# SyncE's reads in program order and apart, and 72 TensorE transposes replaced by transposing reads

## The chip, the cores and the metric

The kernel runs on one core of a Trainium2 chip. The metric is device time in microseconds of one execution; smaller is better. TensorE is called PE, VectorE DVE, ScalarE ACT, GpSimd POOL and SyncE SP, as in the profile.

## The reference

One decoder layer, 256 tokens of width 2048, in float32. Cut to what matters:

```python
h = x + 0.5 * swiglu(rmsnorm(h, ffn1_norm), ffn1_w_gu, ffn1_w_down)
proj = rmsnorm(h, mix_norm) @ w_in                      # columns: gating u, v | z | x, B, C | dt
gu, gv, z, xbc, dt_raw = jnp.split(proj, split_at, axis=-1)
a_out = chunked_sgu(gelu(gu), gelu(gv), ...)            # u * (W_s rmsnorm(v) + b), chunks of 128
xbc = silu(causal_dwconv(xbc, conv_w, conv_b))          # 4 taps
xs, bm, cm = jnp.split(xbc, ...)                        # 32 heads of 64; 8 groups of 128 states
xdt = x * dt[..., None]                                 # inside ssd_scan, chunks of 128
y = ssd_scan(x, dt, a, bm, cm) + d_skip[:, None] * x
m_out = rmsnorm(y * silu(z), norm_w)
h = h + concat([a_out, m_out]) @ w_out
h = h + cross_attention(rmsnorm(h, xa_norm), rmsnorm(mem, mem_norm), w_q, w_kv, w_o)
h = h + 0.5 * swiglu(rmsnorm(h, ffn2_norm), ffn2_w_gu, ffn2_w_down)
return rmsnorm(h, final_norm)
```

## The kernel before

Every weight matrix is streamed from DRAM in tiles of 1 MB (`raw`, 128 x 2048 floats), one per step of the planner. ACT casts a tile to its high part (`hi`), DVE subtracts to get the low part (`lo`), and PE multiplies both by a token operand that is kept in SBUF, in two forms again. Three `raw` buffers and two `lo` buffers go round: a weight read waits for DVE to have finished the tile three steps back, and a low part for PE to have finished the one two steps back. The stages follow one another on PE: FFN 1, the input projection `w_in` (B, C and x columns by `proj_feat`, features on the partitions, 16 + 16 steps of 5.6 us; then v, u and z columns by `proj_tok`, tokens on the partitions, 48 steps of 5.45 us), the output projection `w_out`, cross attention, FFN 2. In `w_out` and the FFNs, pieces of kind "S" share products between sums of operands, so that DVE also forms sums of the weights (`sum`) and of the operand (`forms`, `mts`, `ats`).

Work beside the matmuls is put off by `later(fn, by=n)`: it is issued n steps of the planner later, between two weight steps. PE's instructions, ACT's casts and the low parts on DVE (`split_op`) are each kept in program order; the other instructions are placed on their engine by a scheduler.

Turning an operand (tokens on the partitions to features on the partitions, or back) is done in two ways. Either PE multiplies by the identity (`tpose`, L77) into PSUM, and ACT or DVE copy from there. Or `write_planes` lets ACT split the floats into two planes of 16 bits (`halves`), POOL's queue writes these to DRAM (`planes`), and SP's queue reads them back with a transposing DMA (`turned`, L375). The weight reads stand on SP's queue too, where the scheduler places the transposing reads among them.

The x features come out of the convolution as `xf` (4 multiply-adds on DVE and one product on ACT into `cacc`, then silu on ACT), and are turned to token rows `y0`, `y1` by `x_tokens`. `scan_start` (L875) multiplies y by dt into `xdt` and y by the skip weights; `scan_decay` forms the decays and the scores; `scan_apply` adds PE's `yp` to y. `m_operand` scales y by the norm's factor and turns it into the second half of the operand of `w_out` (`mt`, and `mts` with the sums); `ats.turn_later` does so for the gating output; `Normed.chunk` for the residual stream that the next stage reads (`na` for attention).

Of the kernel before, what the change touches and what calls it, by code (L numbers as in the profile page):

```python
# [47 lines left out]
def hybrid_layer(ctx: ExitStack, tc: tile.TileContext, x, xt, mem, memt, w_gu1, w_dn1, w_in, w_s, w_out,  # L48
# [84 lines left out]
    PLAIN = {(0, 0): 0, (0, 1): 1, (1, 0): 2, (1, 1): 3}  # L133
    FOR_SUMS = {(0, 0): 0, (1, 0): 1, (1, 1): 2, (0, 1): 3}

    def load(w, r0, cs, at, fine=False):
        raw = wraw.tile([P, 2 * KP, NC], F32, name="raw")
        rows = w[r0:r0 + KP * P, :]
        if at is PLAIN and cs[1] == cs[0] + NC:
            nc.sync.dma_start(out=raw.rearrange("p (k j) n -> p k j n", j=2), in_=rows[:, cs[0]:cs[0] + 2 * NC].rearrange(  # L140
                "(k p) (j n) -> p k j n", p=P, j=2))
            return raw
        if fine:
            for (k, j), b in at.items():
                nc.sync.dma_start(out=raw[:, b, :], in_=rows[k * P:(k + 1) * P, cs[j]:cs[j] + NC])
            return raw
        for j, c in enumerate(cs):
            b, e = at[0, j], at[1, j]
            src = rows[:, c:c + NC]
            if e > b:  # L150
                nc.sync.dma_start(out=raw[:, b:e + 1:e - b, :], in_=src.rearrange("(k p) n -> p k n", p=P))
                continue
            for k, x in enumerate((b, e)):
                nc.sync.dma_start(out=raw[:, x, :], in_=src[k * P:(k + 1) * P, :])
        return raw

    def behind(instructions):

        order = ExitStack()
        for ins in instructions:  # L160
            order.enter_context(tc.issue_after(ins))
        return order
# [161 lines left out]
    def proj_feat(w, xts, n0):  # L324
        ps = {}
        n = D // P // (2 * KP)
        for i in range(n):
            raw = wraw.tile([P, 2 * KP, NC], F32, name="raw")
            nc.sync.dma_start(out=raw, in_=w[2 * i * KP * P:2 * (i + 1) * KP * P, n0:n0 + NC].rearrange(
                "(k p) n -> p k n", p=P))  # L330
# [40 lines left out]
            nc.gpsimd.dma_start(out=planes[t * P:(t + 1) * P].rearrange("p b n -> p (b n)"), in_=halves)  # L371
        return planes

    def read_turned(to, planes, c0, n):
        nc.sync.dma_start(out=to, in_=planes[:, :, c0:c0 + n].rearrange("s b n -> (s b) n"), transpose=True)  # L375

    def turn_over(srcs, by, put):
        planes = write_planes(srcs)

        def fetch(q):  # L380
            to = half_k(F32, "turned")
            read_turned(to.bitcast(U16).rearrange("p (k s) -> p k s", k=KP), planes, q * P, KP * P)
            later(lambda: put(to.rearrange("p (k s) -> p k s", k=KP), q), by=by[1], bankless=True)

        for q in (0, 2):
            later(lambda q=q: fetch(q), by=by[0] + q / 4, bankless=True)

    def in_turn(src, last, op, c0=None):

# [66 lines left out]
    class Pieces(dict):  # L456
# [59 lines left out]
                                             op=ALU.subtract)  # L516
            return hi.ins, lo.ins

        def turn_later(self, srcs, by, c0=None, at=None):
            if at is None:  # L520
                at = self.due
                self.due += 2
            turn_over(srcs, by, lambda to, q: self.put(at + q // 2, to, q, c0))

        def later(self, srcs, c0=None, by=1):
            for q in (0, 2):
# [2 lines left out]
    class Normed:  # L529
# [8 lines left out]
        def chunk(self, n, by=1):  # L538
            srcs = [h[n][:, t, :] for t in range(NT)]
            if n < 2 and not isinstance(self.xts, Pieces):  # L540
                operand_turned(srcs, self.xts, f"xt_{self.name}{n}", self.c0 + n * KG, (2.5 + 1.5 * n, 2.5))
                self.stats(n)
            elif isinstance(self.xts, Pieces):

                for i in (2 * n, 2 * n + 1):
                    later(lambda i=i: self.xts.put(i, srcs, i % 2 * KP, self.c0 + n * KG),
                          self.bys.get(i, by))
                later(lambda: self.stats(n), self.stats_by)
            else:
                operand_later(srcs, self.xts, f"xt_{self.name}{n}", self.c0 + n * KG, by)  # L550
                self.stats(n)
# [59 lines left out]
    def ffn(nrm, w_gu, w_dn, done=None, each=None, fine=0, by_token=False):  # L611
        for c_from, c_to in ((0, 5), (5, 11)):
            kinds, turn = DN_KINDS[c_to - c_from]
            hts = Pieces(kinds, "hid", nrm.xts)
            for c in range(c_from, c_to):
                m = {}
                gs = []

                def mid(banks):
                    m["m1"], m["y"], m["z"], m["y2"] = parts_of(banks)  # L620

                def evac(t, j, ps):
                    g, u = (m["z"], m["y2"]) if t else (m["m1"], m["y"])
                    if j == 0:
                        total(g, ps, g, ALU.subtract if t else ALU.add)
                        nc.scalar.activation(g, g, AF.Silu, scale=nrm.rstd[:, t:t + 1])
                        return
                    total(u, ps, u)
                    nc.vector.scalar_tensor_tensor(out=g, in0=u, scalar=nrm.rstd[:, t:t + 1], in1=g,
                                                   op0=ALU.mult, op1=ALU.mult)  # L630
                    gs.append(g)

                if c == 0:
                    proj_sum(w_gu, 0, nrm.xts, FIRST_KINDS, (c * NC, DFF + c * NC), mid, evac, FIRST, fine)
                else:
                    proj_sum(w_gu, 0, nrm.xts, GU_KINDS, (c * NC, DFF + c * NC), mid, evac, GU_ORDER)
                hts.turn_later(gs, (1, 4))
            last = c_to == 11
            add_sum(w_dn, c_from * NC, hts, (kinds, kinds), turn, 0.5, done if last else None, each if last else None,
                    last and by_token)  # L640

# [186 lines left out]
    bt = slot([P, GROUPS, S], F32, "bt")  # L828
    ctr = slot([P, GROUPS, S], F32, "ct")
    def b_tokens(q):  # L830
        ps = side("tpose")
        for i in range(4):
            transpose(out=ps[:, i * P:(i + 1) * P], in_=bt[:, q * 4 + i, :P], identity=ident)
        nc.any.tensor_copy(out=btok[:, q * 4:q * 4 + 4, :], in_=ps.rearrange("p (g n) -> p g n", n=P))

    for c in range(4):
        xis = gather(proj_feat(w_in, nx.xts, B0 + c * NC))
# [3 lines left out]
        for i in range(4):  # L841
            conv_silu(xis[i], 16 + c * 4 + i, dst[:, (c % 2) * 4 + i, :])
        if c < 2:
            later(lambda c=c: b_tokens(c), by=2)
    y = [slot([P, HEADS, HD], F32, f"y{t}") for t in range(NT)]

    def x_tokens(c, i0, xf):
        tps = side("tpose").rearrange("p (t k s) -> p t k s", t=NT, k=2)
        for t in range(NT):
            for i in range(2):  # L850
                transpose(out=tps[:, t, i, :], in_=xf[:, i, t * P:(t + 1) * P], identity=ident)
        for t in range(NT):
# [12 lines left out]

    def per_head(ap, n):
# [5 lines left out]
    def scan_start(t, j):  # L872
        if j == 0:
            scan["xdt"] = scan[f"xdt{t}"] = xdt = slot([P, HEADS, HD], F32, "xdt")
            nc.vector.tensor_tensor(out=xdt, in0=y[t], in1=per_head(dt[:, t, :], HD), op=ALU.mult)  # L875
            nc.vector.tensor_tensor(out=y[t], in0=y[t], in1=per_head(rowb[:, 2, :], HD), op=ALU.mult)
        dec = slot([P, 16, P], F32, "dec")
        nc.gpsimd.dma_start(
# [98 lines left out]
    for c in (0, 2):  # L977
# [41 lines left out]

# [205 lines left out]
```

## Time and profile before

| | before |
|---|---|
| median of 3 runs | 2428.43 us (2428.28 to 2432.98) |
| profiled execution | 2428.32 us, span 2426.6 us |
| PE busy | 2413.6 us, 99% of the span |
| DVE / ACT / POOL busy | 2033.3 / 1361.4 / 65.4 us |
| matmuls on PE | 11141 |
| granted TensorE clock | 0.999 |
| DMA | 510.17 MB, mean 210 GB/s |

The span is the profiled execution without the 1.7 us around it. Busy times are sums of one engine's instructions; PE's matmuls overlap, so that what one costs on PE's path is read from the distance of their starts or from the chain, not from its own duration.

### The profile page before, as it was taken

The numbers are of one execution on the slowest core, as the hardware profiler recorded it, in microseconds if no ns is written. First come the engines' busy times: TensorE is split into PE (matmuls) and PEld (weight loads), VectorE is DVE, ScalarE is ACT, GpSimd is POOL, SyncE is SP. The second block draws the span as 40 slices with busy tenths as digits, with TensorE's granted clock in tenths as the row PEclk, the third lists the DMA queues.
The fourth block names the chain that finished last, engine by engine and source line by source line (L and its number), as shares of the span: only waits on it lengthen the run. The fifth ranks groups of instructions, "written<-read, shape, count | busy, mean of one in ns | idle before, by whom it ended". The sixth has DMA issues, their size and how long they took to land.

```text
span 2426.6 us, 29016 instructions
## 1 busy us (share of the span) xinstructions
PE 2413.6 (99%) x11141; PEld 2010.1 (83%) x11141; DVE 2033.3 (84%) x1943; ACT 1361.4 (56%) x1261; POOL 65.4 (3%) x124
## 2 busy tenths in 40 slices
PE   9999999999999999999999999999999999999998
PEld 7888888888888888788888888888888888888886
DVE  8999889999877777655698888778899988899997
ACT  7565446555656555445555655555556644556554
POOL 1000000000000000000000000000000000000000
PEclk9999999999999999999999999999999999999999
DMA  8777667677765555567557655555567776777774
GB/s 306 234 225 232 202 208 232 220 231 231 232 196 187 181 191 175 205 194 224 190 191 244 224 191 167 176 178 174 191 217 235 225 222 197 223 229 223 233 221 151
DMA packets 264844, 510.17 MB, mean 210 GB/s; under 512 B 75760, under 2 KB 77840, under 8 KB 263936
## 3 DMA queue, kind: packets, MB, share of 16 engines
q1 hardware_dynamic: 256224, 479.00, 62.6%
q0 software_dynamic: 7648, 28.26, 3.2%
q8 instruction: 87, 1.43, 0.2%
q10 hardware_dynamic: 832, 1.05, 0.1%
q14 instruction: 53, 0.43, 0.0%
HBM read 476.76 MB, written 16.81 MB: 203 GB/s over the span
## 4 chain that ended last, share of the span: by engine, by line
PE 95%; issue 3%; ACT 1%; DVE 1%; DMA 0%; SPq 0%; POOL 0%; POOLq 0%; DVEq 0%; ACTq 0%
PE acc L74 92%; PE tpose L77 1%; PE yp L74 1%; PE o L74 0%; PE logits L74 0%; PE mixed L74 0%; DVE lo L177 0%; DMA raw<-in_w_in 0%; ACT hi L169 0%; DMA raw<-in_w_gu 0%; PE dt L74 0%; PE scores L74 0%; PE yo L74 0%; PE st L74 0%; ACT hi L191 0%
## 5 line engine op out<-in xcount | busy, mean ns | idle before, releaser
L177 DVE TENSOR_TENSOR lo<-raw,hi 128x2048 fp32r<-128x2048 f32 (+2 forms) x449 | 945.2, 2107 | 242.5 <-PE acc L74 175.4
L169 ACT CAST hi<-raw 128x2048 fp32r<-128x2048 f32 (+1 forms) x437 | 785.0, 1798 | 488.6 <-PE acc L74 418.4
L74 PE MATMUL acc<-hi,xp_ffn 128*128 128x512 f32 x1824 | 574.3, 390 | 0.0
L74 PEld LDWEIGHTS acc<-hi,xp_ffn 128*128 128x128 f32 x1824 | 342.6, 188 | 71.1
L169 ACT CAST hi<-sum 128x2048 fp32r<-128x2048 f32 x117 | 224.1, 1915 | 294.8 <-DVE sum L177 153.4
L74 PE MATMUL acc<-lo,xp_ffn 128*128 128x512 f32 x912 | 355.0, 389 | 1.3 <-DVE h L661 1.3
L177 DVE TENSOR_TENSOR lo<-sum,hi 128x2048 fp32r<-128x2048 f32 x117 | 268.1, 2292 | 37.4 <-ACT hi L169 37.4
L74 PE MATMUL acc<-hi,hid 128*128 128x512 f32 x896 | 281.3, 389 | 0.0
L74 PE MATMUL acc<-hi,xt_mix 128*128 128x512 f32 x768 | 241.5, 393 | 0.0
L74 PEld LDWEIGHTS acc<-lo,xp_ffn 128*128 128x128 f32 x912 | 171.3, 188 | 37.5 <-DVE h L661 1.7
L600 DVE TENSOR_TENSOR part<-acc,part 128x512 f32<-128x512 f32 x272 | 180.5, 686 | 23.6 <-PE acc L74 8.5
L74 PEld LDWEIGHTS acc<-hi,hid 128*128 128x128 f32 x896 | 168.1, 188 | 34.9
L74 PE MATMUL acc<-lo,hid 128*128 128x512 f32 x448 | 174.3, 389 | 0.0
L74 PEld LDWEIGHTS acc<-hi,xt_mix 128*128 128x128 f32 x768 | 144.2, 188 | 30.8 <-issue 1.0
L177 DVE TENSOR_TENSOR sum<-sum,raw 128x512 f32<-128x512 f32 x234 | 161.6, 691 | 6.2
L74 PE MATMUL acc<-lo,xt_mix 128*128 128x512 f32 x384 | 149.7, 390 | 1.1 <-DVE lo L177 1.1
L74 PE MATMUL acc<-hi,xp_ffn1s 128*128 128x512 f32 x466 | 148.5, 389 | 0.0
L74 PE MATMUL acc<-hi,xp_ffn2s 128*128 128x512 f32 x466 | 148.5, 389 | 0.0
L177 DVE TENSOR_TENSOR sum<-raw 128x1024 f32<-128x1024 f32 x117 | 142.5, 1218 | 0.0
L74 PE MATMUL acc<-xt_mix,hi 128*128 128x512 f32 x512 | 140.5, 396 | 0.0
L74 PE MATMUL acc<-hi,hids 128*128 128x512 f32 x392 | 125.2, 389 | 0.0
L74 PE MATMUL acc<-hi,memt 128*128 128x512 f32 x384 | 123.4, 392 | 0.0
(297 smaller groups left out, 3164.6 us busy)
## 6 DMA issues: line engine op xcount, KB each, us to landing
raw<-in_w_gu SPq DMA_DIRECT2D x284, 512.0 KB, 4.6
raw<-in_w_in SPq DMA_DIRECT2D x80, 1024.0 KB, 5.1
raw<-in_w_dn SPq DMA_DIRECT2D x60, 1024.0 KB, 5.2
raw<-in_w_gu SPq DMA_DIRECT2D x136, 256.0 KB, 4.9
raw<-in_w_kv SPq DMA_DIRECT2D x24, 1024.0 KB, 5.2
raw<-in_w_out SPq DMA_DIRECT2D x21, 1024.0 KB, 5.2
planes<-halves POOLq DMA_DIRECT2D x56, 256.0 KB, 4.6
raw<-in_w_dn SPq DMA_DIRECT2D x28, 512.0 KB, 4.1
```

The source lines that it names most:

```text
L74: return pe(nc.tensor.matmul(out, lhsT=lhsT, rhs=rhs, start=start, stop=stop))
L77: return pe(nc.tensor.transpose(out=out, in_=in_, identity=identity))
L169: last_cast[:] = [nc.scalar.copy(out=t[:, :n], in_=x[:, :n]).ins]
L177: last_split[:] = [nc.vector.tensor_tensor(**kw).ins]
L600: nc.vector.tensor_tensor(out=out, in0=a, in1=b, op=op)
```

## The change

`from_dram` takes the place of SP's plain DMA calls. From the first down projection of FFN 1 on, each of its "lined" reads (weights, and transposing reads of the operands of the input projection, the output projection and attention) is chained behind the last, so that SP has them in program order; the reads of the FFNs' operands, of B and of y are not in that line. Two transposing reads of one operand, put off by a quarter of a step per 128 columns before (two reads half a step apart), now come one step apart, and the reads come due 6 and 8 steps after the planes instead of 2.5 and 4, with the use one step after the read instead of 2.5.

B (8 transposes), the x features (32), the chunks 2 and 3 of the scan's output (16) and the chunks 0 and 1 of the residual stream for attention (16) are turned through planes in DRAM instead of on PE. The scan's parts are put off by 1 to 1.5 steps more, and `xdt` joins the ordered line of low parts on DVE.

```diff
+    def from_dram(lined=True, **kw):
+        with behind(last_load if lined and line["kept"] else ()):
+            ins = nc.sync.dma_start(**kw).ins
+        if lined:
+            last_load[:] = [ins]
...
-    def turn_over(srcs, by, put):
+    def turn_over(srcs, by, put, lined=True):
...
-            later(lambda q=q: fetch(q), by=by[0] + q / 4, bankless=True)
+            later(lambda q=q: fetch(q), by=by[0] + (q / 2 if lined else q / 4), bankless=True)
...
-                operand_turned(srcs, self.xts, f"xt_{self.name}{n}", self.c0 + n * KG, (2.5 + 1.5 * n, 2.5))
+                operand_turned(srcs, self.xts, f"xt_{self.name}{n}", self.c0 + n * KG, (6 + 2 * n, 1))
                 self.stats(n)
+            elif n < 2 and self.name == "xa":
+                self.xts.turn_later(srcs, (6 + 2 * n, 1), self.c0 + n * KG, 2 * n)
+                later(lambda: self.stats(n), self.stats_by)
...
     def b_tokens(q):
-        ps = side("tpose")
-        for i in range(4):
-            transpose(out=ps[:, i * P:(i + 1) * P], in_=bt[:, q * 4 + i, :P], identity=ident)
-        nc.any.tensor_copy(out=btok[:, q * 4:q * 4 + 4, :], in_=ps.rearrange("p (g n) -> p g n", n=P))
+        planes = dram.tile([P, 2, NC], U16, name="planes", tag="planes", bufs=4)
+        halves = tmp.tile([P, 2 * NC], U16, name="halves", tag="t2k")
+        halves_v = halves.rearrange("p (b g n) -> p b g n", b=2, g=4)
+        for g in range(4):
+            nc.scalar.copy(out=halves_v[:, :, g, :],
+                           in_=bt[:, q * 4 + g, :P].bitcast(U16).rearrange("p (n b) -> p b n", b=2))
+        nc.gpsimd.dma_start(out=planes.rearrange("p b n -> p (b n)"), in_=halves)
+        later(lambda: read_turned(btok[:, q * 4:q * 4 + 4, :].bitcast(U16), planes, 0, NC, False), by=1, bankless=True)
...
     def x_tokens(c, i0, xf):
-        tps = side("tpose").rearrange("p (t k s) -> p t k s", t=NT, k=2)
-        for t in range(NT):
-            for i in range(2):
-                transpose(out=tps[:, t, i, :], in_=xf[:, i, t * P:(t + 1) * P], identity=ident)
-        for t in range(NT):
+        planes = write_planes([xf[:, i, :] for i in range(2)], S)
+
+        def fetch(t):
             h0 = (c * 4 + i0) * 2
-            nc.any.tensor_copy(out=y[t][:, h0:h0 + 4, :],
-                               in_=tps[:, t].rearrange("p k (h d) -> p (k h) d", d=HD))
+            read_turned(y[t][:, h0:h0 + 4, :].bitcast(U16).rearrange("p h d -> p (h d)"), planes, t * P, P, False)
+
+        for t in range(NT):
+            later(lambda t=t: fetch(t), by=1 + 2 * t, bankless=True)
...
-            later(lambda c=c, i0=i0, xf=xf: x_tokens(c, i0, xf), by=2 + i0 // 2)
+            x_tokens(c, i0, xf)
...
-            nc.vector.tensor_tensor(out=xdt, in0=y[t], in1=per_head(dt[:, t, :], HD), op=ALU.mult)
+            split_op(out=xdt, in0=y[t], in1=per_head(dt[:, t, :], HD), op=ALU.mult)
...
-    for i, (by, to) in enumerate(((3, 8), (8, 12), (14, 18.5), (18.5, 23))):
+    for i, (by, to) in enumerate(((4.5, 9), (9, 13), (15, 19.5), (19.5, 24))):
...
-            ats.turn_later(gss[j], (2.5 + 1.5 * j, 2.5))
+            ats.turn_later(gss[j], (6 + 2 * j, 1))
...
-        mts.later(gs, C_SSM + c * KG)
+        if c < 2:
+            mts.later(gs, C_SSM + c * KG)
+        else:
+            mts.turn_later(gs, (c + 3, 1), C_SSM + c * KG, 2 * c)
...
-        later(lambda c=c: m_operand(c), by=1 + c)
+        later(lambda c=c: m_operand(c), by=(1, 2, 1.5, 2.5)[c], bankless=c > 1)
```

How the instructions move is shown at three places. In the rows, a name's number tells one buffer's use from another's, and the brackets hold what an instruction waits for.

First, DVE at the scan's start, in the first v steps of `w_in`. `cacc` are the convolution's multiply-adds of the last x features, the four `lo` those of the v steps 34 to 37. Before:

```order
L177 TENSOR_TENSOR lo_7079<-raw_7075,hi_7077 128x2048 [waits DMAHW3_49,PE_49]
L747 SCALAR_TENSOR_TENSOR cacc_6992<-hi_5243,col_96,cacc_6992 128x256 [waits Activation_49]
L747 SCALAR_TENSOR_TENSOR cacc_6992<-hi_5243,col_96,cacc_6992 128x256 [waits DVE_49] x2
L177 TENSOR_TENSOR lo_7121<-raw_7117,hi_7119 128x2048 [waits DMAHW4_49,PE_49]
L854 COPY y0_6170<-tpose_7068 128x256 [waits PE_49]
L177 TENSOR_TENSOR lo_7151<-raw_7147,hi_7149 128x2048 [waits DMAHW5_49,PE_49,Activation_49]
L854 COPY y0_6170<-tpose_7105 128x256 [waits PE_49]
L875 TENSOR_TENSOR xdt_7112<-y0_6170,dt_5259 128x2048 [waits DVE_49]
L876 TENSOR_TENSOR y0_6170<-y0_6170,rowb_103 128x2048 [waits DVE_49]
L177 TENSOR_TENSOR lo_7191<-raw_7187,hi_7189 128x2048 [waits DMAHW6_49,PE_49,Activation_49]
```

And after:

```order
L185 TENSOR_TENSOR lo_7136<-raw_7132,hi_7134 128x2048 [waits DMAHW2_49,PE_49]
L759 SCALAR_TENSOR_TENSOR cacc_7008<-hi_5243,col_96,cacc_7008 128x256 [waits DVE_49]
L759 SCALAR_TENSOR_TENSOR cacc_7015<-hi_5243,col_96,cacc_7015 128x256 [waits DMASW5_49,DMASW4_49,Activation_49]
L759 SCALAR_TENSOR_TENSOR cacc_7015<-hi_5243,col_96,cacc_7015 128x256 [waits DVE_49] x2
L185 TENSOR_TENSOR lo_7166<-raw_7162,hi_7164 128x2048 [waits DMAHW3_49,PE_49]
L185 TENSOR_TENSOR xdt_7192<-y0_6174,dt_5259 128x2048 [waits DMAHW5_49,DMAHW1_49,DMAHW0_49]
L185 TENSOR_TENSOR lo_7201<-raw_7197,hi_7199 128x2048 [waits DMAHW4_49,PE_49,Activation_49]
L892 TENSOR_TENSOR y0_6174<-y0_6174,rowb_103 128x2048 [waits DVE_49]
L185 TENSOR_TENSOR lo_7231<-raw_7227,hi_7229 128x2048 [waits DMAHW7_49,PE_49,Activation_49]
```

The last multiply-adds now stand behind `lo_7136`, the low part of step 35, and `xdt`, which waited for DVE's own copies, waits for transposing reads of y0 (DMAHW) ahead of the low part of step 37, `lo_7201`. The reads that it waits for stand so on SP after the change (before, only the weight reads stand there):

```order
L147 DMA raw_7197<-in_w_in 128x2x1024 [waits DMAHW7_49,DVE_49,Activation_49]
L147 DMA_TRANSPOSE y0_6174<-planes_6999 128x512 [waits DMAHW5_49,DMASW6_49,DMASW5_49]
L147 DMA_TRANSPOSE y1_6175<-planes_6999 128x512 [waits DMAHW6_49]
L147 DMA raw_7227<-in_w_in 128x2x1024 [waits DMAHW2_49,DVE_49,Activation_49]
L147 DMA raw_7267<-in_w_in 128x2x1024 [waits DMAHW0_49,DMAHW3_49,DVE_49,Activation_49]
L147 DMA_TRANSPOSE y0_6174<-planes_7021 128x512 [waits DMAHW1_49,DMASW7_49,DMASW0_49]
L147 DMA_TRANSPOSE y1_6175<-planes_7021 128x512
L147 DMA raw_7309<-in_w_in 128x2x1024 [waits DMAHW4_49,DVE_49]
```

The last read of y0 comes behind the weight read of step 39, `raw_7267`.

Second, SP's queue in the z steps, where the operands of the gating output are read. Before:

```order
L140 DMA raw_8467<-in_w_in 128x2x1024 [waits DMAHW7_49,DMAHW2_49,DVE_49]
L375 DMA_TRANSPOSE turned_8399<-planes_8290 128x2x512 [waits DMASW4_49,DMASW3_49,Activation_49]
L375 DMA_TRANSPOSE turned_8401<-planes_8290 128x2x512 [waits Activation_49]
L375 DMA_TRANSPOSE turned_8433<-planes_8297 128x2x512 [waits DMASW6_49,DMASW5_49,Activation_49]
L375 DMA_TRANSPOSE turned_8465<-planes_8297 128x2x512
L140 DMA raw_8509<-in_w_in 128x2x1024 [waits DMAHW0_49,DVE_49]
```

And after:

```order
L147 DMA_TRANSPOSE turned_8509<-planes_8303 128x2x512 [waits DMAHW5_49,DMASW6_49]
L147 DMA raw_8511<-in_w_in 128x2x1024 [waits DMAHW2_49,DVE_49]
L147 DMA_TRANSPOSE turned_8541<-planes_8303 128x2x512 [waits DMAHW7_49]
L147 DMA raw_8552<-in_w_in 128x2x1024 [waits DMAHW3_49,DVE_49]
L147 DMA_TRANSPOSE turned_8605<-planes_8310 128x2x512 [waits DMASW7_49,DMASW0_49,DVE_49]
L147 DMA raw_8607<-in_w_in 128x2x1024 [waits DMAHW4_49]
L147 DMA_TRANSPOSE turned_8650<-planes_8310 128x2x512 [waits DVE_49]
L147 DMA raw_8652<-in_w_in 128x2x1024 [waits DMAHW6_49]
```

The four transposing reads stood together; now a weight read stands behind each.

Third, DVE in the first pass of `w_out`, with the operand's third and fourth groups (`forms`, `mts`, `mt`) and the shared pieces (`sum`). Before, these groups come in the plain pieces, the last ahead of the first shared piece's end:

```order
L177 TENSOR_TENSOR lo_9178<-raw_9168,hi_9176 128x1536 [waits PE_49]
L509 TENSOR_TENSOR forms_9121<-forms_9118 128x256 [waits Activation_49]
L515 TENSOR_TENSOR mts_9112<-forms_9118,mts_9112 128x512 [waits PE_49,Activation_49]
L511 TENSOR_TENSOR forms_9121<-forms_9118,forms_9121 128x128 [waits DVE_49]
L417 SCALAR_TENSOR_TENSOR mt_9072<-tpose_9129,col_96,mt_9072 128x256 [waits PE_49,Activation_49]
L512 TENSOR_TENSOR forms_9121<-forms_9118,forms_9121 128x128 [waits DVE_49]
L417 SCALAR_TENSOR_TENSOR mt_9072<-tpose_9129,col_96,mt_9072 128x256
L177 TENSOR_TENSOR lo_9182<-sum_9172,hi_9180 128x2048 [waits Activation_49]
```

And after, the third group in the second shared piece:

```order
L185 TENSOR_TENSOR lo_9196<-raw_9192,hi_9194 128x2048 [waits DMAHW5_49,PE_49]
L517 TENSOR_TENSOR forms_9228<-forms_9225 128x256 [waits DMASW4_49,DMASW0_49]
L185 TENSOR_TENSOR sum_9240<-raw_9236 128x1024 [waits DMAHW1_49,DMAHW7_49,DMAHW0_49,DVE_49]
L519 TENSOR_TENSOR forms_9228<-forms_9225,forms_9228 128x128 [waits DVE_49]
L185 TENSOR_TENSOR sum_9240<-sum_9240,raw_9236 128x512 [waits DVE_49]
L520 TENSOR_TENSOR forms_9228<-forms_9225,forms_9228 128x128 [waits DVE_49]
L185 TENSOR_TENSOR sum_9240<-sum_9240,raw_9236 128x512 [waits DVE_49]
L185 TENSOR_TENSOR lo_9246<-raw_9236,hi_9244 128x1536 [waits PE_49,Activation_49]
L523 TENSOR_TENSOR mts_9224<-forms_9228,mts_9224 128x512 [waits Activation_49]
L185 TENSOR_TENSOR lo_9250<-sum_9240,hi_9248 128x2048 [waits Activation_49]
L425 SCALAR_TENSOR_TENSOR mt_9273<-turned_9210,col_96,mt_9273 128x256 [waits DMAHW6_49,Activation_49]
```

The operand's work now lies between the sums and low parts of the shared pieces, and its input comes from a transposing read (`turned_9210`) instead of PSUM.

More of the change, by code (lines that the diff above doesn't have):

```diff
@@ L134, in hybrid_layer, with behind @@
     FOR_SUMS = {(0, 0): 0, (1, 0): 1, (1, 1): 2, (0, 1): 3}
+    def behind(instructions):
+        order = ExitStack()
+        for ins in instructions:
+            order.enter_context(tc.issue_after(ins))
+        return order
+    line, last_load = {"kept": False}, []
+    def from_dram(lined=True, **kw):
[3 more added lines that the diff above has]
+            last_load[:] = [ins]
     def load(w, r0, cs, at, fine=False):
@@ L139, in load @@
         if at is PLAIN and cs[1] == cs[0] + NC:
-            nc.sync.dma_start(out=raw.rearrange("p (k j) n -> p k j n", j=2), in_=rows[:, cs[0]:cs[0] + 2 * NC].rearrange(
+            from_dram(out=raw.rearrange("p (k j) n -> p k j n", j=2), in_=rows[:, cs[0]:cs[0] + 2 * NC].rearrange(
                 "(k p) (j n) -> p k j n", p=P, j=2))
@@ L144, in load @@
             for (k, j), b in at.items():
-                nc.sync.dma_start(out=raw[:, b, :], in_=rows[k * P:(k + 1) * P, cs[j]:cs[j] + NC])
+                from_dram(out=raw[:, b, :], in_=rows[k * P:(k + 1) * P, cs[j]:cs[j] + NC])
             return raw
@@ L150, in load @@
             if e > b:
-                nc.sync.dma_start(out=raw[:, b:e + 1:e - b, :], in_=src.rearrange("(k p) n -> p k n", p=P))
+                from_dram(out=raw[:, b:e + 1:e - b, :], in_=src.rearrange("(k p) n -> p k n", p=P))
                 continue
             for k, x in enumerate((b, e)):
-                nc.sync.dma_start(out=raw[:, x, :], in_=src[k * P:(k + 1) * P, :])
+                from_dram(out=raw[:, x, :], in_=src[k * P:(k + 1) * P, :])
         return raw
[L157 to L162, printed above, removed]
     last_cast = []
@@ L328, in proj_feat @@
             raw = wraw.tile([P, 2 * KP, NC], F32, name="raw")
-            nc.sync.dma_start(out=raw, in_=w[2 * i * KP * P:2 * (i + 1) * KP * P, n0:n0 + NC].rearrange(
+            from_dram(out=raw, in_=w[2 * i * KP * P:2 * (i + 1) * KP * P, n0:n0 + NC].rearrange(
                 "(k p) n -> p k n", p=P))
@@ L372, in write_planes, with read_turned @@
         return planes
-    def read_turned(to, planes, c0, n):
-        nc.sync.dma_start(out=to, in_=planes[:, :, c0:c0 + n].rearrange("s b n -> (s b) n"), transpose=True)
-    def turn_over(srcs, by, put):
+    def read_turned(to, planes, c0, n, lined=True):
+        from_dram(lined, out=to, in_=planes[:, :, c0:c0 + n].rearrange("s b n -> (s b) n"), transpose=True)
+    def turn_over(srcs, by, put, lined=True):
         planes = write_planes(srcs)
@@ L381, in fetch @@
             to = half_k(F32, "turned")
-            read_turned(to.bitcast(U16).rearrange("p (k s) -> p k s", k=KP), planes, q * P, KP * P)
+            read_turned(to.bitcast(U16).rearrange("p (k s) -> p k s", k=KP), planes, q * P, KP * P, lined)
             later(lambda: put(to.rearrange("p (k s) -> p k s", k=KP), q), by=by[1], bankless=True)
         for q in (0, 2):
-            later(lambda q=q: fetch(q), by=by[0] + q / 4, bankless=True)
+            later(lambda q=q: fetch(q), by=by[0] + (q / 2 if lined else q / 4), bankless=True)
     def in_turn(src, last, op, c0=None):
@@ L517, in sums, with turn_later @@
             return hi.ins, lo.ins
-        def turn_later(self, srcs, by, c0=None, at=None):
+        def turn_later(self, srcs, by, c0=None, at=None, lined=True):
             if at is None:
@@ L522, in turn_later @@
                 self.due += 2
-            turn_over(srcs, by, lambda to, q: self.put(at + q // 2, to, q, c0))
+            turn_over(srcs, by, lambda to, q: self.put(at + q // 2, to, q, c0), lined)
         def later(self, srcs, c0=None, by=1):
@@ L636, in ffn @@
                     proj_sum(w_gu, 0, nrm.xts, GU_KINDS, (c * NC, DFF + c * NC), mid, evac, GU_ORDER)
-                hts.turn_later(gs, (1, 4))
+                hts.turn_later(gs, (1, 4), lined=False)
             last = c_to == 11
+            line["kept"] = True
             add_sum(w_dn, c_from * NC, hts, (kinds, kinds), turn, 0.5, done if last else None, each if last else None,
@@ L843, in hybrid_layer @@
         if c < 2:
-            later(lambda c=c: b_tokens(c), by=2)
+            b_tokens(c)
     y = [slot([P, HEADS, HD], F32, f"y{t}") for t in range(NT)]
     def x_tokens(c, i0, xf):
-        tps = side("tpose").rearrange("p (t k s) -> p t k s", t=NT, k=2)
+        planes = write_planes([xf[:, i, :] for i in range(2)], S)
+        def fetch(t):
+            h0 = (c * 4 + i0) * 2
+            read_turned(y[t][:, h0:h0 + 4, :].bitcast(U16).rearrange("p h d -> p (h d)"), planes, t * P, P, False)
         for t in range(NT):
-            for i in range(2):
-                transpose(out=tps[:, t, i, :], in_=xf[:, i, t * P:(t + 1) * P], identity=ident)
-        for t in range(NT):
-            h0 = (c * 4 + i0) * 2
-            nc.any.tensor_copy(out=y[t][:, h0:h0 + 4, :],
-                               in_=tps[:, t].rearrange("p k (h d) -> p (k h) d", d=HD))
+            later(lambda t=t: fetch(t), by=1 + 2 * t, bankless=True)
     for c in range(4):
```

## Prediction

> **What bounds the kernel now.** I read the page's busy times first, then the chain of work that ended last, the windows, and what TensorE waited for.
>
> ```profile
> PE 2413.6 (99%) x11141; PEld 2010.1 (83%) x11141; DVE 2033.3 (84%) x1943; ACT 1361.4 (56%) x1261; POOL 65.4 (3%) x124
> PE 95%; issue 3%; ACT 1%; DVE 1%; DMA 0%; SPq 0%; POOL 0%; POOLq 0%; DVEq 0%; ACTq 0%
> 0.00:30.00 30.00, 27.46 (x109) 22.04 (x110) 22.88 (x45) 25.05 (x43) 4.92 (x14) 1.00 0.98 344
> 30.00:2400.00 2370.00, 2368.86 (x10958) 1974.15 (x10958) 1993.57 (x1873) 1328.35 (x1205) 58.26 (x107) 1.00 0.66 210
> 2400.00:2426.60 26.60, 17.26 (x77) 13.95 (x75) 16.84 (x27) 7.97 (x15) 2.25 (x4) 0.87 0.21 79
> PE acc L74 <- DVE lo L177: 1.1, 1, 1.1
> ```
>
> The first row gives each engine's busy time, the second the chain by engine. The three windows read: length, then busy time of PE, PEld, DVE, ACT and POOL, granted clock, DMA share, GB/s. Between 30 and 2400 us PE is idle for 2370.00 - 2368.86 = 1.14 us, and the last row names that: one wait for a low part made by VectorE. The start and the end, which the change does not touch, hold the other 2.5 + 9.3 us. So the time is PE's own work: what leaves PE is won in full, as long as no new wait opens, and any new wait is lost in full.
>
> **Transposes that leave PE.** From the diff: 8 of the B features, 32 of the x features, 16 of the scan output (two of four chunks), 16 of the attention norm's state: 72 in all. What one costs on PE's path is read from the chain (start, length, what), not from its own duration of 272 ns, because matmuls overlap.
>
> ```profile
> 734.90 0.44 PE tpose L77 x4
> 874.43 0.44 PE tpose L77 x4
> 1199.57 0.87 PE tpose L77 x8
> 1275.00 1.75 PE tpose L77 x16
> ```
>
> 0.44/4, 0.87/8 and 1.75/16 all give 0.109 us. 72 x 0.109 = 7.85 us; the matmul after a group may lose a little of that to its own start, so I take 7.7 and keep 7.3 to 7.9.
>
> **The one wait that goes.** In the gating stage four transposing reads stand together on SyncE's queue, and the weight read behind them is late. Chain rows, after the queue's row:
>
> ```profile
> 1102.59 11.62 SPq L375 DMA_TRANSPOSE turned<-planes  x4
> 1112.92 1.29 SPq L375
> 1114.31 6.18 DMA raw<-in_w_in
> 1120.59 1.91 ACT hi L169
> 1125.23 2.30 DVE lo L177
> 1127.57 2.57 PE acc L74 x10
> ```
>
> The four reads hold the queue from 1102.59 to 1114.21; the weights behind land at 1120.48, are split, and PE takes their low part at 1127.57, 1.1 us late. Now a weight read stands between any two of these reads, so one turned read is all that a weight read can be behind. I put this at -1.1 (0 if the chain of waits merely shifts).
>
> **What the reads cost elsewhere.** Added: 26 transposing reads on SyncE (16 of half size for y, 2 for B, 4 for the scan's output, 4 for the attention state), 26 plane writes on GpSimd, some 32 copies on ScalarE; 18 PSUM copies of y and B go. Rows (ns or us, minimum/median/maximum; the second row is of the transposing reads, the fourth of the plane writes):
>
> ```profile
> L375 SPq DMA_TRANSPOSE turned<-planes x56: 1226/1290/4759, 61.3 to 2302.7; - x56
> DMA to landing us min/median/max: 3.0/4.1/8.8
> L371 POOL DMA_DIRECT2D planes<-halves x56: 539/540/627, 57.6 to 2298.1; - x56
> DMA to landing us min/median/max: 2.3/4.6/8.2
> L369 ACT COPY halves<-part x44: 1035/1046/1052, 56.2 to 2296.8; 128x1024 uint16<-128x1024 uint16 x44
> 876.00:935.00 59.00, 59.00 (x301) 50.08 (x300) 44.10 (x40) 33.13 (x43) 0.00 (x0) 1.00 0.56 186
> 1040.00:1140.00 100.00, 98.86 (x442) 81.88 (x442) 58.38 (x52) 52.93 (x49) 4.33 (x8) 1.00 0.76 221
> 1196.00:1236.00 40.00, 40.00 (x190) 33.41 (x189) 38.86 (x50) 25.42 (x32) 0.00 (x0) 1.00 0.57 184
> ```
>
> GpSimd's 26 x 0.54 = 14 us lie on an engine at 3%. ScalarE's copies (8 of 1.05, 16 of half length, 8 short, about 22 us less some 7 of copies that go) lie beside its 56%: near the end of the x features it has idle time in front of every cast, and the casts are released by PE (a buffer comes free), not by a DMA:
>
> ```profile
> 880.01 1.91 ACT L169 CAST hi<-raw 128x2048 fp32r<-128x2048 f32 x1 [3.08 <-PE acc L74]
> 903.38 1.91 ACT L169 CAST hi<-raw 128x2048 fp32r<-128x2048 f32 x1 [3.26 <-PE acc L74]
> ```
>
> So weights already wait there, and a weight read may come two reads' issue (2 x 1.29 = 2.6 us) later. If that cover went, a read at 4.76 us each would delay weights by 9.5 us against about 3 us here and the cast's own lead over PE. Cost taken: 0. The reads of the gating, scan-output and attention operands come due 3 to 8 steps of 5.45 us after their planes are written (16 us against the longest landing of 8.2), so no weight read waits in line for planes; B is turned some forty steps before the states use it; the scan's parts, due 1 to 1.5 steps later, still end 8 steps before the z columns begin. These cost nothing.
>
> **A new wait at the scan's start.** Before, the multiply xdt needed y from a PSUM copy on VectorE itself. Now it waits for the last transposing read of y0, and the low part of weight step 37, y0's own multiply and the low part of step 38 stand behind it on VectorE. PE waits for the low parts. Rows of VectorE before, and PE's first use of step 37:
>
> ```profile
> 895.66 1.52 DVE L747 SCALAR_TENSOR_TENSOR cacc<-hi,col,cacc 128x256 f32<-128x256 f32 x3
> 897.10 2.28 DVE L177 TENSOR_TENSOR lo<-raw,hi 128x2048 fp32r<-128x2048 f32 x1
> 897.22 0.51 ACT L749 ACTIVATE xf<-cacc,col 128x256 f32<-128x256 f32 x1 [2.10 <-DVE cacc L747]
> 902.98 2.29 DVE L177 TENSOR_TENSOR lo<-raw,hi 128x2048 fp32r<-128x2048 f32 x1 [3.26 <-issue]
> 905.64 2.29 DVE L875 TENSOR_TENSOR xdt<-y,dt 128x2048 f32<-128x2048 f32 x1
> 910.17 2.29 DVE L177 TENSOR_TENSOR lo<-raw,hi 128x2048 fp32r<-128x2048 f32 x1
> 914.69 0.89 PE scores L74 x8
> 915.65 0.40 PE L74 MATMUL acc<-lo,xt_mix 128*128 128x512 f32 x1
> ```
>
> On the clock of these rows: in the new order the convolution's last four steps come behind the low part at 897.10, not ahead of it. That ends at 899.3; then one step, ScalarE's silu (0.5) and first product (0.5), three steps (1.5): 902.5. Silu 0.5 and a half-length copy, between 0.5 and 1.05, say 0.6: 903.6. Plane write 4.6: 908.2. Transposing read 3.0 to 4.1: 911.2 to 912.3. xdt 2.2 and the low part 2.3: 915.7 to 916.8. PE wants the low part at 915.65 less 8 transposes (0.9) that go and the scores (0.9) that now come later: 913.9. Wait: 1.8 to 2.9 us, I take 2.2, near the low end, since a half-size read should land sooner than the full-size ones in the row. With the shortest write and read (2.3, 3.0) it is 0; with the longest (8.2, 8.8) it is 3.6 + 4.7 over the 2.9, 11.2.
>
> A page speaks against the change here: the Trainium skill, "VectorE: DVE Perf Modes", section "Rules for kernel authors", says to transpose 128x128 on TensorE where a PSUM destination will do, and its section "The three transpose paths" gives 390 ns there against 1309 ns by DMA. By those two figures 72 transposes would cost 66 us more, an estimate that holds only if every one lay on the path; the chain's 0.109 us and the row of 1290 ns for one read's issue agree with the order of the two, and the trace has slack for all but the reads at the scan's start.
>
> **VectorE in the output projection.** From 1196 to 1236 us VectorE is busy 38.86 of 40 (last window above). Two of the four groups of m operands move from there to the shared pieces that follow, where a pair of pieces looks so:
>
> ```profile
> 1238.83 2.29 DVE L177 TENSOR_TENSOR lo<-raw,hi 128x2048 fp32r<-128x2048 f32 x1 [0.89 <-PE acc L74]
> 1245.77 2.29 DVE L177 TENSOR_TENSOR lo<-sum,hi 128x2048 fp32r<-128x2048 f32 x1 [0.39 <-ACT hi L169]
> 1249.03 2.29 DVE L177 TENSOR_TENSOR lo<-raw,hi 128x2048 fp32r<-128x2048 f32 x1 [0.97 <-PE acc L74]
> 1214.65 0.42 DVE L509 TENSOR_TENSOR forms<-forms 128x256 f32<-128x256 f32 x1
> 1216.78 2.28 DVE L177 TENSOR_TENSOR lo<-sum,hi 128x2048 fp32r<-128x2048 f32 x1
> 1218.98 0.68 DVE L515 TENSOR_TENSOR mts<-forms,mts 128x512 fp32r<-128x512 f32 x1
> ```
>
> One pair (1238.83 to 1249.03) has 0.39 + 0.97 = 1.36 us free. A group takes 1216.78 - 1214.65 = 2.1, and its last operation 0.6 more: 2.7. Each of two pairs is 1.4 short, 2.7 together. Against that stands the lead of the low parts over PE: the idle for PE in these rows says that VectorE waits for PE to free a buffer, so it is ahead by most of a piece's 5 us less its own 2.3. I take 0.4; ends 0 and 2.7.
>
> **Sum**, on the profiled execution of 2428.32 us (span 2426.6; the median of the runs is 2428.43, 0.1 above): -7.7 -1.1 +2.2 +0.4 = -6.2, so 2422.1.
>
> **Rivals.**
> - No new wait: write and read near their minima, the pieces in time. 2428.3 - 7.8 - 1.1 = 2419.4. For it: minimum rows of 2.3 and 3.0, half-size transfers, DMA share only 0.56. Against it: the path above misses by 2 us at medians.
> - The gain is mostly spent: the wait at the scan's start at 4 to 5 us (a copy or write in line behind other work on ScalarE or GpSimd) and 1 to 2.7 in the output projection. 2428.3 - 8.9 + 5.0 to 7.7 = 2424.4 to 2427.1. For it: VectorE at 97% there; the chain has seven links, each of which can only be late.
> - Slower than before: the last y0 read meets a full queue, so the write takes 8.2 and the read 8.8. Wait 11.2: 2428.3 - 8.9 + 11.2 = 2430.6, and 2433.3 if VectorE's 2.7 in the output projection is paid as well. It decides from 8.9 us of wait on. The Trainium skill's rule above would show here, as a read's latency put on the path. Against it: such rows come where the DMA share is 0.76; at this place it is 0.56, and the added reads would raise it to about 0.7 by estimate (four of some 128 KB and their writes in 22 us, beside 4 weight reads of 1 MB).
> - The reads do not keep apart, and the 1.1 us stays: 2423.2, still inside the forecast.
>
> **Chances.** My case, 2420.4 to 2423.6: 0.42. No new wait: 0.21. Mostly spent: 0.26. Full queue: 0.08, half of it past 2433. Something that I did not see in the other reads: 0.03. Apart from no change a measurement here tells about 0.2%, 4.9 us: faster means under 2423.6, slower over 2433.3. Faster 0.42 + 0.21 = 0.63; slower 0.05; the rest, 0.32, within. The range runs from 2418 (no new wait, and something under the transposes' own pitch) to 2427.5 (mostly spent), leaving out the full queue and the unseen.
>
> **What would show it.** PE's matmuls fewer by 72, its busy time near 2405.8; no wait at 1127. A wait of PE or its weight loads for a low part about 27 us after the first v step, with xdt ahead of it on VectorE, released by a DMA. That y0 read's landing 3 to 4 us after its issue. In the output projection, VectorE without idle in the pieces 8 to 11. I am wrong if that wait is over 4 us, if weight reads become late in the x features (casts released by a DMA), or if PE has new idle time in any other stage.

## The result and the profile after

| | before | after |
|---|---|---|
| median | 2428.8 us (2428.28 to 2432.98, 4 runs) | 2456.13 us (2455.5 to 2460.32, 4 runs) |
| ratio to before | | 1.0112, 95% interval 1.0095 to 1.013 |
| span of the profiled execution | 2426.6 us | 2454.2 us |

The change makes the kernel 27 us slower, where 6 us faster were forecast. The page after, its busy times and the chain by engine:

```profile
span 2454.2 us, 28974 instructions
PE 2413.3 (98%) x11069; PEld 2006.8 (82%) x11069; DVE 2032.6 (83%) x1941; ACT 1376.2 (56%) x1277; POOL 83.3 (3%) x150
PE 87%; issue 9%; DMA 1%; DVE 1%; ACT 1%; POOL 0%; SPq 0%; POOLq 0%; DVEq 0%; ACTq 0%
```

PE has 72 matmuls fewer and yet the same busy time, 2413.3 against 2413.6 us. So two things went wrong: PE is idle for 2454.2 - 2413.3 = 40.9 us instead of 13.0, and what work is left takes longer. What PE waited for (total, times, longest):

```profile
PE acc L74 <- ACT hi L177: 16.9, 2, 9.8
PE acc L74 <- DVE lo L185: 12.3, 6, 7.5
```

And where, with the granted clock (windows of the changed kernel; behind the window: its length, busy PE, PEld, DVE, ACT, POOL, clock, DMA share, GB/s):

```profile
30.00:2400.00 2370.00, 2341.05 (x10764) 1948.34 (x10764) 1971.31 (x1859) 1328.41 (x1213) 76.67 (x133) 0.99 0.66 212
900.00:1000.00 100.00, 92.21 (x443) 77.67 (x443) 66.50 (x42) 50.73 (x54) 2.70 (x6) 0.97 0.59 197
1100.00:1200.00 100.00, 79.13 (x324) 63.78 (x325) 45.27 (x35) 46.14 (x43) 2.16 (x4) 0.90 0.59 192
1200.00:1260.00 60.00, 59.95 (x274) 49.55 (x273) 45.76 (x54) 39.35 (x48) 3.01 (x5) 1.00 0.76 223
```

Of the 28.9 us of idle between 30 and 2400 us (1.1 before), 7.8 lie at the scan's start and 20.9 in the z steps, where the gating output's operands are read. The output projection, where 0.4 us were forecast, has 0.05. The two stages are also those with a clock below 1.00.

**The z steps.** SP's queue there, first in time order (start, length, what), then what it waited for between 1050 and 1170 us:

```profile
1086.01 1.23 SPq L147 DMA_TRANSPOSE turned<-planes  x1
1087.29 0.57 SPq L147 DMA_DIRECT2D raw<-in_w_in  x1
1104.41 1.30 SPq L147 DMA_TRANSPOSE turned<-planes  x1
1105.76 15.74 SPq L147 DMA_DIRECT2D raw<-in_w_in  x5
...
1131.30 0.37 SPq L147 DMA_DIRECT2D raw<-in_w_in  x1
1157.13 1.23 SPq L147 DMA_TRANSPOSE turned<-planes  x1
1158.41 0.57 SPq L147 DMA_DIRECT2D raw<-in_w_in  x1
```

```profile
SPq L147 <- DVE y L1016: 25.6, 2, 25.4
SPq L147 <- DMA planes<-halves: 16.5, 1, 16.5
```

A transposing read held the queue for 16.5 us until 1104.41, and another for 25.4 us until 1157.13, and every weight read stood behind it. (Before the first of them, the read at 1086.01 had waited 11.0 us for DVE's use of an earlier `turned`.) Neither of the two waited for its own data, whose planes had been written tens of microseconds before. Each waited for the place that it writes to. `turned` comes from one pool of six buffers (`half_k`) that `gate`, `halves`, `forms`, `xf`, `junk` and others share in turn. With the reads due 6 to 9 steps after the planes, the last two of four come behind the next group of gates, 8 steps later, in that turn. The buffer of the read at 1104.41 had been one of `halves` of the next gates (its plane write landed at 1104.36), that of the read at 1157.13 one of the z gates (DVE's use, L1016, ended at 1157.10). Those gates are made from the last products of the running weight steps: SP could go on only after PE had finished those steps. ScalarE at the first of the two places:

```profile
1099.57 1.26 ACT L999 ACTIVATE gate<-acc,rstd_mix 128x512 f32<-128x512 f32 x2 [1.45 <-PE acc L74]
1100.73 4.27 ACT L377 COPY halves<-gate 128x1024 uint16<-128x1024 uint16 x4
1104.91 1.89 ACT L177 CAST hi<-raw 128x2048 fp32r<-128x2048 f32 x1
1114.06 1.91 ACT L177 CAST hi<-raw 128x2048 fp32r<-128x2048 f32 x1 [6.74 <-DMA raw<-in_w_in]
```

The weights of step 64 had landed, but their cast stands behind the gates and the four copies on ScalarE (1104.91); those of step 65 were read only at 1105.76 and are cast at 1114.06. And PE there:

```profile
1099.15 0.61 PE L74 MATMUL acc<-hi,xt_mix 128*128 128x512 f32 x2
1106.85 0.79 PE L74 MATMUL acc<-hi,xt_mix 128*128 128x512 f32 x1 [7.09 <-ACT hi L177]
1109.18 0.79 PE L74 MATMUL acc<-lo,xt_mix 128*128 128x512 f32 x1 [1.53 <-DVE lo L185]
1109.77 0.63 PE L74 MATMUL acc<-hi,xt_mix 128*128 128x512 f32 x1
1110.20 0.63 PE L74 MATMUL acc<-lo,xt_mix 128*128 128x512 f32 x1
...
1114.52 0.39 PE L74 MATMUL acc<-hi,xt_mix 128*128 128x512 f32 x1
```

Two waits, 7.09 and 1.53 us, and behind them matmuls start 0.43 us apart for some 4 us, against 0.23 otherwise.

**The scan's start.** DVE of the changed kernel:

```profile
897.06 1.01 DVE L759 SCALAR_TENSOR_TENSOR cacc<-hi,col,cacc 128x256 f32<-128x256 f32 x2 [4.45 <-ACT cacc L757]
903.08 2.28 DVE L185 TENSOR_TENSOR lo<-raw,hi 128x2048 fp32r<-128x2048 f32 x1
914.44 2.29 DVE L185 TENSOR_TENSOR xdt<-y,dt 128x2048 f32<-128x2048 f32 x1 [9.07 <-DMA raw<-in_w_in]
916.65 2.28 DVE L185 TENSOR_TENSOR lo<-raw,hi 128x2048 fp32r<-128x2048 f32 x1
```

The place is as forecast: xdt waits (the last y0 read landed at 914.36), the low part of step 37 stands behind it, and PE takes it at 918.99, 7.5 us late. The bracket in xdt's row names a weight read, which landed at 913.88; xdt does not wait for that one but, by the order rows, for the reads of y0. The y reads' landing and SP's queue:

```profile
DMA to landing us min/median/max: 2.4/2.7/5.5
885.21 2.42 SPq L147 DMA_TRANSPOSE y<-planes  x2
887.73 4.39 SPq L147 DMA_DIRECT2D raw<-in_w_in  x3
900.20 2.43 SPq L147 DMA_TRANSPOSE y<-planes  x2
902.73 3.08 SPq L147 DMA_DIRECT2D raw<-in_w_in  x2
908.84 2.54 SPq L147 DMA_TRANSPOSE y<-planes  x2
```

Each pair of y reads goes the moment its planes have landed (885.16, 900.14, 908.82): SP had come to them before (between 820 and 915 us it waited 39.5 us for plane writes), and the weight reads stood behind. And ScalarE, on which the convolution's products wait behind the cast of a late weight tile:

```profile
893.65 1.91 ACT L177 CAST hi<-raw 128x2048 fp32r<-128x2048 f32 x1 [4.17 <-DMA raw<-in_w_in]
```

### The profile page after: what moved, and what is told of

Its sections match the earlier page's. It is cut to its first block, busy times and chain, and to the rows that moved or that the text cites. A ratio compares the mean times of both kernels' runs of the same rounds, so it can differ in the third digit from the quotient of the medians.

```text
span 2454.2 us, 28974 instructions
## 1 busy us (share of the span) xinstructions
PE 2413.3 (98%) x11069; PEld 2006.8 (82%) x11069; DVE 2032.6 (83%) x1941; ACT 1376.2 (56%) x1277; POOL 83.3 (3%) x150
## 4 chain that ended last, share of the span: by engine, by line
PE 87%; issue 9%; DMA 1%; DVE 1%; ACT 1%; POOL 0%; SPq 0%; POOLq 0%; DVEq 0%; ACTq 0%
PE acc L74 84%; DMA raw<-in_w_in 1%; PE tpose L77 1%; PE yp L74 1%; DVE lo L185 1%; PE o L74 0%; PE logits L74 0%; ACT hi L177 0%; DVE cacc L759 0%; ACT halves L377 0%; PE mixed L74 0%; DMA planes<-halves 0%; DMA raw<-in_w_gu 0%; PE dt L74 0%; SPq L147 0%
```

## The experiments

The theory: SP's queue is in order, and a read that waits holds the weights behind it, whether it waits for its planes or for its buffer; the new idle is that, and the clock behind the idle is low. The rivals: the transposing reads' own DMA load; the line; the place of xdt alone.

| kernel | edit to the changed kernel | median us | ratio to before, 95% interval |
|---|---|---|---|
| e1 | no line | 2441.45 | 1.0052, 1.0037 to 1.0067 |
| e2 | gating reads due early, as before | 2438.16 | 1.0033, 1.002 to 1.0047 |
| e3 | x features on PE | 2450.12 | 1.0086, 1.0069 to 1.0103 |
| e4 | e2 and e3 | 2433.08 | 1.0016, 1.0007 to 1.0026 |
| e5 | gating reads due between, x features on PE | 2422.22 | 0.9974, 0.9964 to 0.9984 |
| e9 | gating reads due between | 2427.0 | 0.9994, 0.9984 to 1.0003 |
| e7 | gating reads due between, scan later | 2419.27 | 0.9961, 0.9948 to 0.9975 |
| e10 | e7 without the line | 2419.07 | 0.9955, 0.9942 to 0.9967 |
| e8 | no line, no spacing, early, scan later | 2422.62 | 0.9976, 0.9966 to 0.9985 |
| e11 | e7 and six waits put in | 2457.88 (one run) | |

**e1, the line taken away.**

```diff
-            line["kept"] = True
+            line["kept"] = False
```

> The changed kernel with the line taken away: SP's reads are no longer chained, all else (due times, transposes on DMA) stays. Theory (head of line: in the gating and z stages a weight read stands on SP behind a transposing read that waits for a buffer which only the end of the previous group of gates frees): the scheduler puts weight reads ahead of the waiting reads again, the 20.9 us of idle PE between 1100 and 1200 us go, and with them about 6 us of low PE clock behind the idle: 2429 us. The 7.8 us at the scan's start stay. Rival (the transposing reads take DMA time that the weights need, wherever they stand): about 2450 to 2456 us, idle PE at the same places.

Measured 2441.45: half of the loss went, not all. Between 1100 and 1200 us 8.2 us of idle are left. The weights now land in time (step 65 at 1089), but their cast does not come: ScalarE,

```profile
1102.14 0.62 ACT L416 CAST at<-turned 128x512 fp32r<-128x512 f32 x1 [0.49 <-DMA turned<-planes]
1102.67 1.99 ACT L377 COPY halves<-gate 128x1024 uint16<-128x1024 uint16 x2
1104.56 1.89 ACT L177 CAST hi<-raw 128x2048 fp32r<-128x2048 f32 x1
```

has the cast of step 65 behind a late operand and the gates' copies. The waiting read does damage in two queues, and the line is only one of them. The rival, DMA load, would have left all of it.

**e2 and e3, one wait each, and e4, both.**

```diff
# e2
-            ats.turn_later(gss[j], (6 + 2 * j, 1))
+            ats.turn_later(gss[j], (2.5 + 1.5 * j, 2.5))
# e3: x_tokens as before the change, and
-            x_tokens(c, i0, xf)
+            later(lambda c=c, i0=i0, xf=xf: x_tokens(c, i0, xf), by=2 + i0 // 2)
```

> The changed kernel with the gating output's transposing reads due 2.5 and 4 steps after their planes, as before the change, in place of 6 and 8; the line stays. Theory (head of line, by the buffer): the reads are issued before the next group of gates takes the buffers, so they do not wait, and the line costs nothing: 2429 us. If the program order alone, and not the late due time, were the cause: idle PE stays near 20 us and the time near 2455 us.

> The changed kernel with the x features turned on PE as before (32 transposes back, 16 reads of y and 16 plane writes gone). Theory: the 7.8 us of idle PE at the scan's start go, and about 1.5 us of low clock; 3.5 us of transposes come back: 2450 us. The idle in the gating and z stages stays at about 21 us. Rival (the wait at the scan's start comes from something other than the reads of y, such as the later due times or the place of xdt): no change of that idle, and 2459 us by the transposes.

> Both edits: the gating reads due at 2.5 and 4 steps, the x features on PE. Theory: no idle PE but at the start and the end, no low clock behind it, 40 transposes fewer than before the change (4.4 us) and the 1.1 us wait of before gone: 2423 us. If the two waits hide one another, or a third is behind them: 2428 us or more.

e3 came out as expected (2450.12 for 2450), with no wait of PE at the scan's start: that wait comes with the y reads. e2 and e4 fell short, by 9 and 10 us (e2's runs lie between 2433.33 and 2439.63, and its trace is of the fastest). With the early due time SP comes to the read before its planes have landed. In e4:

```profile
1056.47 1.29 SPq L147 DMA_TRANSPOSE turned<-planes  x1
1057.81 0.57 SPq L147 DMA_DIRECT2D raw<-in_w_in  x1
1058.48 5.39 SPq L147 DMA_TRANSPOSE turned<-planes  x2
1063.92 0.57 SPq L147 DMA_DIRECT2D raw<-in_w_in  x1
```

```profile
SPq L147 <- DMA planes<-halves: 38.3, 3, 21.5
```

For up to 21.5 us SP stands before a transposing read (second fence: SP's waits of e4 between 1040 and 1130 us), and the weights behind come late by 1.8 us once and 1.6 + 1.8 us the second time. So in line there is a due time too early (planes not landed) and one too late (buffer not free), as far as PE is concerned.

**e5, due between, and e9, that alone.** e5 is e3 and e9 is the changed kernel, both with

```diff
-            ats.turn_later(gss[j], (6 + 2 * j, 1))
+            ats.turn_later(gss[j], (4 + 2 * j, 1))
```

> As e4 (x features on PE, line kept), but the gating reads due 4, 5, 6 and 7 steps after their planes, neither 2.5 to 5 nor 6 to 9: late enough that the planes have landed when SP comes to the read (in e4 a weight read stood behind a transposing read that waited for its plane write, 1.8 us and 3.4 us of idle PE), early enough that they come ahead of the next group of gates in the use of buffers. Theory (head of line): no idle PE between 30 and 2400 us, no low clock, 40 transposes fewer: 2429.0 - 4.4 - 1.1 = 2423.5 us. Rival (DMA load of four reads among the weight reads makes the weights late wherever they stand): idle as in e4, 2431 to 2433 us.

> The changed kernel with only the gating reads moved, due 4 to 7 steps after their planes; the scan's due times stay. Theory (two separate waits, each followed by a stretch of low clock): the gating part goes whole, 20.9 us of idle and about 6 us of low clock, and the scan's start stays, 7.8 + 1.8 us over e7's 2419.3: 2429 us. If the two were coupled (the late scan pushes the gating reads, or the other way): off by more than 3 us from that.

e5: 2422.22, idle PE in the z steps none. That settles the gating part: with all the gating reads in place, two steps decide over 20 us (e3 against e5, 27.9), so their DMA load is not it. e9: 2427.0, so the due time alone takes 29.1 us off the 2456.1, and its one remaining wait is that of the scan:

```profile
PE acc L74 <- DVE lo L185: 5.9, 1, 5.9
```

SP still stands before a read in e9, for up to 15.8 us; what differs is how many weights have been read ahead of it. The read that waits until 1104.41 in the changed kernel has weights up to step 64 ahead of it, the one that waits until 1104.68 in e4 up to step 66, the one that waits until 1105.31 in e9 up to step 67. All three wait for work on the gates of step 63; only in e9 does PE not have to wait.

**e7, the scan later as well.**

```diff
-    for i, (by, to) in enumerate(((4.5, 9), (9, 13), (15, 19.5), (19.5, 24))):
+    for i, (by, to) in enumerate(((7.0, 11.5), (11.5, 15.5), (17.5, 22.0), (22.0, 26.5))):
```

> The changed kernel, all 72 transposes by DMA and the line kept, with two times moved: the gating reads due 4 to 7 steps after their planes, and the scan's parts 2.5 steps later, so that xdt stands behind the low parts of steps 37 and 38 on DVE. SP's order of the y reads is the same as in the changed kernel. Theory: y0 has landed when DVE comes to xdt, or the wait falls behind low parts that PE has already; no idle PE, no low clock: 2429.0 - 7.8 - 1.1 = 2420 us. Rival (the weight reads that stand behind y reads on SP make PE wait by themselves): idle of 1 to 4 us near 895 to 915 us, and with its low clock 2423 to 2428 us.

2419.27: xdt now stands behind the low parts of steps 37 and 38, and its wait falls on nobody. It is the fastest kernel, with e10, 0.4% under before. Its page, PE's one wait between 30 and 2400 us, and SP's waits for planes between 1040 and 1170 us, which cost PE nothing:

```profile
PE 2406.1 (100%) x11069; PEld 2002.1 (83%) x11069; DVE 2032.1 (84%) x1941; ACT 1376.3 (57%) x1278; POOL 83.4 (3%) x150
```

```profile
PE acc L74 <- DVE lo L185: 0.2, 1, 0.2
SPq L147 <- DMA planes<-halves: 24.7, 3, 13.7
```

PE's busy time is 7.5 us under that of before: the price of 72 transposes.

**e10 and e8, what the line is worth.** e10 is e7 with the edit of e1; e8 is that with the early due times and the quarter steps of before the change.

> e7 without the line (gating reads due 4 to 7, scan 2.5 steps later, SP's reads unchained). If the line gives something where no read waits: 2421 to 2423 us, since the scheduler puts the gating reads in groups of four and a wait of about 1 us with or without low clock comes back. If the due times alone carry it: 2419 to 2420 us, as e7.

> The 72 transposes by DMA without the line and without the spacing: SP's reads unchained, the gating reads due at 2.5 and 4 steps and half a step apart as before the change, the scan's parts 2.5 steps later as in e7. If the transposes alone carry the gain: 2421 to 2422 us, with a wait of about 1 us in the z steps as before the change. If the line is needed for it: 2424 us or more, waits behind groups of transposing reads.

e10 is as fast as e7: where no wait of SP reaches PE, the line gives nothing. e8 is 3.4 us slower than e7, with one wait of 2.0 us in the z steps where before the change had 1.1. Without the line the early reads do little harm (e8), with it they cost 16 us more (e2, from which some 8 us are the scan's; e8 also lacks the spacing, and no run parts the two).

**e11, the price of idle.** After the low part of six z steps, DVE writes it again, so many whole and quarter times:

```diff
+    again = {34: (2, 0), 36: (2, 1), 38: (2, 2), 42: (3, 0), 44: (4, 0), 46: (6, 0)}
...
+            for b in [2 * KP] * whole + [1] * quarter:
+                split_op(out=lo[:, :b], in0=raw[:, :b], in1=hi[:, :b].bitcast(F32), op=ALU.subtract)
```

> A probe of what an idle PE costs beyond the idle: e7, in which the low part of six z steps is written again 2, 2.25, 2.5, 3, 4 and 6 times over by VectorE, so that PE waits some 0.8, 1.4, 2.0, 3.0, 5.2 and 9.6 us at steps that have no other wait (the repeats write the same values). If an idle of over some 1.2 us by itself brings a stretch at half the TensorE clock: 22 us of idle and 1.7 us more behind each of the last four or five, 2449 us. If the low clock came from something else in the stages of the changed kernel (its DMA load): 2441 us and matmuls 227 ns apart right after each wait.

2457.88, more than expected, since the waits came out longer (0.97, 3.2, 2.9, 4.2, 5.6 and 10.3 us). The page's busy time and PE's waits:

```profile
PE 2417.5 (98%) x11069; PEld 2010.2 (82%) x11069; DVE 2076.9 (85%) x1963; ACT 1376.9 (56%) x1278; POOL 83.4 (3%) x150
```

```profile
PE acc L74 <- DVE lo L185: 27.2, 6, 10.3
```

27.2 us of idle, and PE 2417.5 - 2406.1 = 11.4 us longer at the same matmuls: 2419.3 + 27.2 + 11.4 = 2457.9. The window around the wait of 4.2 us:

```profile
1157.00:1161.85 4.85, 0.65 (x4) 0.19 (x2) 4.82 (x4) 2.51 (x3) 0.00 (x0) 1.00 0.00 0
1161.85:1163.85 2.00, 2.00 (x6) 1.62 (x7) 2.00 (x1) 0.00 (x0) 0.00 (x0) 0.71 0.42 57
1163.85:1165.85 2.00, 2.00 (x6) 1.57 (x5) 0.14 (x1) 0.00 (x0) 0.00 (x0) 0.50 1.00 387
1165.85:1168.00 2.15, 2.15 (x10) 1.71 (x10) 0.00 (x0) 0.00 (x0) 0.00 (x0) 0.94 0.99 381
```

The clock (the last number but two) falls to half behind the wait, for some 3 to 4 us, with no change but the repeated low parts. So the low clock of the changed kernel is the idle's own.

## Why the prediction was wrong, point by point

- **The transposes that leave PE: right.** Forecast 7.7 us; PE's busy time falls by 7.5 (e7 against before).
- **The wait of before: right, and of no use.** The 1.1 us at 1127 went, but the reads that had caused it now wait themselves.
- **"so no weight read waits in line for planes ... These cost nothing": the step that failed.** It asked whether the data was there and not whether the place was. One of the last two reads of each four waited, 16.5 and 25.4 us, for a buffer held by gates, or by the halves made of them, and these depend on PE's current weights. The order rows of the z steps did show such waits, for DVE and others behind the name of the read, and I took them as met. Worth 29.1 us by e9. In the profiled executions (2454.2 - 2425.2 = 29.0) PE is idle for 23.8 us less, of which 1.6 are the scan's shorter wait, and busy for 5.2 us less.
- **The scan's start: mechanism right, size wrong.** Forecast 2.2 with ends 0 and 11.2; the wait was 7.5 (5.9 in e9, where it cost 7.7, e9 against e7). Two links of the chain were mis-sized. The last read landed 5.5 us after its issue, not 3.0 to 4.1. And the convolution, which I put on the clock of before, did not come earlier with PE, which had shed all of the 32 x transposes by then, 3.5 us and not 0.9: the weight tile of step 35 came late and held ScalarE for 4.17 us. On the trace the low part of step 37 is ready at 918.95, 2.9 us behind the forecast's 913.9 + 2.2 = 916.1 (2.1 of it the read), and PE wants it at 911.5, 2.4 us ahead of the 913.9. This division is read from the trace alone; no run parts the two. (The steps listed up to 902.5 add up to 902.3.)
- **"Cost taken: 0", in the x features: the second term that failed.** Weights came late there and casts were released by a DMA, the sign that was named as one of failure. The term counted the issue of two y reads, 2.6 us, and not their wait for planes, for which SP stood 39.5 us in all. Nor did ScalarE have idle time "in front of every cast" before: the two rows are of casts that had, while those at 874.37, 886.05 and 897.63 follow on other work.
- **Low clock: not in the sum at all.** The prediction's "any new wait is lost in full" was too little: more than the wait is lost. Between the spans of the changed kernel and e7, 2454.2 and 2417.8, lie 36.4 us: 29.2 of idle (40.9 against 11.7) and 7.2 of PE's busy time (2413.3 against 2406.1) for the same number of matmuls.
- **The output projection: forecast 0.4, measured 0.05.** VectorE's hand count of 2.7 against its lead was pessimistic; the pieces kept it.
- **The rival that ended slower** placed the harm at the scan's start by full-queue prices. Most of the harm, 20.9 of 28.9 us of idle, came in the stage that I had booked as a gain. The rule of the Trainium skill, "VectorE: DVE Perf Modes", section "Rules for kernel authors", to transpose on TensorE, would have given the right sign here for another reason: e7 with all 72 by DMA is the fastest kernel.

## What to carry to other kernels

A DMA that waits on an in-order queue costs what stands behind it, so of every moved transfer ask two questions: when is its data there, and who used its buffer before it. In a pool that is shared in turn, moving a step later in the program moves it behind other users of that pool, and if one of them depends on what stands in the queue, the pipeline drains. Then ask a third: how much has been read ahead of it when it comes to wait. The safe place is late enough that what stands ahead lasts until the data has landed, and early enough that the next user has not been allocated, here steps 4 to 7 out of 8; find it from the trace before changing the order, since the order itself gave nothing.

## What the runs showed of the hardware

From some length on, an idle of PE costs more than itself. Waits of 0.97 (e11), 1.14 (before) and 1.16 us (after) left matmuls 0.23 us apart; from 1.8 us on (e4 and e2 at their first wait in the z steps) they start 0.43 us apart behind the wait, 6 to 14 of them, 1.4 to 2.9 us lost each time, whether the idle was 2.9 or 10.3 us. No wait standing alone between 1.2 and 1.8 us was measured. In the traces' own record of the clock, each stretch at 0.5 between 30 and 2395 us lasts 3.41, 6.83, 10.24 or 17.07 us. The Trainium skill, "TensorE: Matmul & The Clock Gate", section "Part 1: The HAM clock gate (the "warmup" mystery)", states two clocks, full and half, a fall after at least one idle window of about 3.4 us, and 3.4 us of work to come back, in windows that run free of the kernel. The half clock, its length and its scatter agree with these runs; the idle that is enough does not: 1.8 us sufficed here.
